# Padding small tiles of a two-layer decoder trunk so that its matmul operands start at multiples of 512 bytes

## The chip, the core and the metric

The kernel runs on one core of one Trainium2 chip. The metric is the device time of one execution in microseconds; less is better. Before the change it is 2253.3 us, the median of 3 runs (2253.23 to 2253.68).

## What is computed

Two layers of a decoder on 256 tokens with 2048 features, all inputs and outputs fp32. Layer 0 mixes tokens with sparse attention ("NSA"), layer 1 with gated linear attention ("GLA"); each is followed by an MLP with a hidden width of 8192.

```python
def squared_relu_mlp(h, w_up, w_down):
    return jnp.square(jax.nn.relu(h @ w_up)) @ w_down

def reference(x, ...):
    for i in range(DEPTH):                      # DEPTH = 2
        h = rms_norm(x, norm_mix[i])
        y = nsa_mixer(h, ...) if i == 0 else gla_mixer(h, ...)
        x = x + y
        h = rms_norm(x, norm_mlp[i])
        x = x + squared_relu_mlp(h, mlp_w_up[i], mlp_w_down[i])
    return x
```

Every mixer begins with one wide projection (h @ w_in) and ends with another (@ w_out). These projections and the MLPs are the "dense products"; what lies between them (scores, softmax, decays, transposes) is small.

## The kernel before

**Precision.** A dense product of fp32 numbers is made from three products of a shorter fp32 form (the type F32R): each operand is split into a high part and a low part, and high by high, high by low and low by high are summed in PSUM. The split of a weight tile is a copy on ScalarE (`wh`) and a subtraction on VectorE (`wl`), lines 194 and 198; the activations `op` (and the hidden activations `ht` of the MLP) lie in SBUF with the high and the low part side by side.

**Stages and loops.** In time: NSA projections with the attention worked in between (`mode_a`: the activations are stationary, 512 weight columns move, three matmuls for each 128 rows and 128 tokens); the NSA output projection (`out_proj`: weights stationary, 256 activation columns move); the first MLP (`mode_b` with `wide`: weights stationary; one matmul moves 512 columns, the high and the low part of the activations, and one moves 256); then GLA's projections, its output projection and the second MLP in the same forms. The MLP takes its 8 chunks of hidden features in turn: up 0, up 1, down 0, up 2, down 1, and so on. The hidden activations of the even chunks lie in tiles `ht` of the pool `mlpz`, those of the odd chunks in tiles `op` of the pool `opool`.

**Order.** All instructions are issued in an order that a planner in the program (`Plan`) fixes when the program is built: the dense products are the main line, and the steps of attention and of the norms step in between them. The weights come through the queue of SyncE in loads of 1 MB, three of them in flight (`raw`).

**Where tiles lie.** Pools lie in each partition of SBUF in the order in which they are opened, and tiles of a pool one behind the other; every tile starts at a multiple of 32 bytes. In bytes from the start of a partition the order is: constants (`cid` at 16512, 768 bytes; `mhalf` at 17280), `xpool` (the residual stream `xs`), `opool` (7 tiles `op`), `wraw` (`raw`), `wsp` (`wh`, `wl`), `small` (vectors such as `rstd`), `zpool`, and behind that the pools of a layer (`mlpz`, or `nsa1` and `nsa2`, or `gla1` and `gla2`). `mhalf` is 8 fp32 wide, 32 bytes, so that `xs0` begins at 17312, which is 33 * 512 + 416. All tiles of `xpool`, `opool`, `wraw` and `wsp` are whole multiples of 512 bytes long, so all of them begin 416 bytes behind a multiple of 512.

The lines that issue every product of the main line:

```python
    def mm(dst, lhsT, rhs, **kw):
        ...
        nc.tensor.matmul(dst, lhsT, rhs, skip_group_check=True, **kw)
```

`lhsT` is the stationary operand, which is loaded into the array by an instruction of its own (LDWEIGHTS, engine PEld in the profile), and `rhs` the moving one. Each matmul has its own weight load.

Of the kernel before, what the change touches and what calls it, by code (L numbers as in the profile page):

```python
# [10 lines left out]
F32 = mybir.dt.float32  # L11
# [7 lines left out]
P = 128  # L19
T = 256  # L20
# [11 lines left out]
class Plan:  # L32
    """Order of emission, which every engine keeps. The dense products are the main line; side
    streams (generators) step in between their matmuls. A stream yields (time, resources): when
    its next step's operands are there, by the plan's clocks, and the slots this step takes."""
# [10 lines left out]
    # -- operands  # L46
# [16 lines left out]
    # -- slots of the pools  # L63
# [17 lines left out]
    # -- streams  # L81
# [32 lines left out]
    def wait(self, needs):  # L114
        """For the main line: let the streams give slots back."""
        while not all(sum(f < 1e12 for f in self.slots[tag]) >= n for tag, n in needs.items()):
            self.tick(1e9)
            self.t["pe"] += 50.0
# [3 lines left out]
def trunk_kernel(ctx: ExitStack, tc: tile.TileContext, a: dict, out: bass.AP):  # L122
# [108 lines left out]
    def evac_splits(items):  # L231
        """evac_split of several, whose low parts don't hold up the vector engine."""
        for hi, lo, src, scale in items:
            if scale is None:
                copy(hi, src)
            else:
                act(hi, src, AF.Copy, scale=scale)
        yield W.ready(items[-1][0])
        for hi, lo, src, scale in items:
            if scale is None:  # L240
                tt(lo, src, hi.bitcast(F32), ALU.subtract)
            else:
                stt(lo, src, scale, hi.bitcast(F32), ALU.mult, ALU.subtract)
# [19 lines left out]
    def slotted(pool, tag, n):  # L263
        """An allocator of a pool's slots which the plan knows of."""
        W.pool(tag, n)

        def alloc(shape, dtype=F32):
            t = pool.tile(list(shape), dtype, tag=tag, name=nm(tag), bufs=n)
            W.take(tag, t)
            return t  # L270
        return alloc
# [12 lines left out]
    mhalf = const.tile([P, 8], F32, name="mhalf")  # L284
    nc.gpsimd.memset(mhalf, -0.5)
    # the scalar engine's table and the tensor engine's clock, while the first loads are under way
    idle = zpool.tile([P, T], F32, tag="junk", name="idle")
    nc.vector.memset(idle, 0.0)
    copy(mhalf[:, 7:8], mhalf[:, 0:1])
# [4 lines left out]
    # by features: [128, tokens] each  # L294
    xs = [xpool.tile([P, T], F32, name=f"xs{n}") for n in range(KT)]

# [1 line left out]
    class Weights:  # L298
        AHEAD = 2
        # when the plan expects the first half units  # L300
# [109 lines left out]
    # the first two units of an MLP: first halves before second ones  # L410
# [11 lines left out]
    def mode_a(op, ps, kts, before=None):  # L422
        """ps[t] = sum over kts of x^T(kt)[tok, :] @ w(kt); a half unit holds 2 kt."""
        k0, k1 = kts[0], kts[-1]
        for i in range(0, len(kts), 2):
            pair = kts[i:i + 2]
            if before is not None:
                for kt in pair:
                    before(kt)
            hi, lo = weights.next()  # L430
            for t in range(NT):
                for j, kt in enumerate(pair):
                    wh = hi[:, j * 512:(j + 1) * 512]
                    wl = lo[:, j * 512:(j + 1) * 512]
                    o = op[kt // 4]
                    xh = o[:, kt % 4, 0, t * P:(t + 1) * P]
                    xl = o[:, kt % 4, 1, t * P:(t + 1) * P]
                    mm(ps[t], xh, wh, start=(kt == k0), stop=False)
                    mm(ps[t], xh, wl, start=False, stop=False)
                    mm(ps[t], xl, wh, start=False, stop=(kt == k1))  # L440
                    if t == 0 and j == 1:
                        weights.lows()
                    W.tick()
                    weights.early()

    def mode_b(op, steps, wide, before=None, slack=2500.0):
        """A half unit, 8 of w(kt)^T @ x(kt) for 128 features each; wide: the low parts' products
        in ps[:, T:]. Steps: kt, ps, first and last of its sum."""
# [18 lines left out]
    def out_proj(oTs, after, ready):  # L467
        """Halves of K; in them blocks of 8 features, whose sums take two turns of 4 kt each."""
# [24 lines left out]
    def gate_product(op):  # L493
        """[96, T]: products with the weights' high and low parts in turn."""
# [18 lines left out]
    def transposed(src, cols):  # L513
        """A bank [128, 2, NT, 128] with the transposes of two column blocks of src [128, NT, 512]."""
        pt = aux([P, 2, NT, P])
        for j, c in enumerate(cols):
            for t in range(NT):
                transpose(pt[:, j, t, :], src[:, t, c:c + P], ident)
        return pt

    class Prep:
        """Gained operand of the next phase, and the tokens' mean squares."""
# [50 lines left out]
        def rstd(self):  # L573
            """Per token, which are on the partitions."""
# [10 lines left out]
            r = small.tile([P, NT], F32, tag="rstd", name=nm("rstd"))  # L585
# [3 lines left out]
    def mlp(prep, after, last):  # L589
        op = prep.op  # L590
        with tc.tile_pool(name="mlpz", bufs=2) as zp:
# [4 lines left out]
            def factors():  # L596
                """1 / mean square of every token, on all partitions."""
# [85 lines left out]
    # ================= layer 0: NSA =================  # L683
    def nsa(prep, after):
        op = prep.op
        G, HPG = 4, 4
        with tc.tile_pool(name="nsa1", bufs=1) as s1, tc.tile_pool(name="nsa2", bufs=1) as s2:
# [7 lines left out]
            def tables():  # L695
                """Constants, and the rope tables with the gains: (cos*g, swapped sin*g)."""
# [12 lines left out]
                gcol = s1.tile([P, 4], F32, name="gcol")  # L709
# [8 lines left out]
                vsel = s1.tile([48, 2], F32, name="vsel")  # L718
# [23 lines left out]
            def factors():  # L742
                rstd = yield from prep.rstd()
                # rstd^2 / 128, rstd / 2
                r2d = s1.tile([P, NT], F32, name="r2d")
                tt(r2d, rstd, rstd, ALU.mult)
                ts(r2d, r2d, 1.0 / P, None, ALU.mult)
                rhalf = s1.tile([P, NT], F32, name="rhalf")
# [3 lines left out]
            # columns: first tokens' selection and window keys, compressed ones, the other tokens'  # L752
# [10 lines left out]
            def normed(dst, ps):  # L763
                """dst = heads of 128 over their rms (with the tokens' factors)."""
# [39 lines left out]
            def keys(ps, g0):  # L804
                """A block of keys: selection and window branch of the groups g0 and g0 + 1."""
# [23 lines left out]
            def compress(ps, which):  # L829
# [18 lines left out]
                def fetch(u):  # L848
                    # u in turn into a slot of either pool
# [9 lines left out]
                for u in range(4):  # L859
# [16 lines left out]
                    # high and low parts side by side, of the weights and of the blocks  # L876
# [80 lines left out]
                else:  # L957
                    # rows 0..16 and 32..48: high part; rows 16..32: low part
# [57 lines left out]
            def attend(g, h, qT, oT):  # L1016
# [19 lines left out]
                # per query and branch: largest score, negated  # L1036
# [11 lines left out]
                # p: [cmp 16, 16 | sel 0, win 0 of the first tokens | sel 0, win 0, sel 1, win 1 of the others]  # L1048
# [38 lines left out]
                # compressed branch: high, high, low parts side by side  # L1087
# [7 lines left out]
                # transposed probabilities: [sel0 256 | win0 256], [sel1 128 | win1 128 | cmp 256]  # L1095
# [68 lines left out]
    # ================= layer 1: GLA =================  # L1164
    def gla(prep, after):
        op = prep.op
        NLEV = 8
        with tc.tile_pool(name="gla1", bufs=1) as s1, tc.tile_pool(name="gla2", bufs=1) as s2:
# [10 lines left out]
            onorm = s1.tile([P, 4], F32, name="onorm")  # L1179
# [7 lines left out]
            # blocks of 64 tokens: the high parts on one half of the partitions, the low parts on the other  # L1187
# [18 lines left out]
            def factors():  # L1206
                rstd = yield from prep.rstd()
                rq = s1.tile([P, NT], F32, name="rq")
                ts(rq, rstd, 1.0 / 16.0, None, ALU.mult)
                rhalf = s1.tile([P, NT], F32, name="rhalf2")  # L1210
# [3 lines left out]
            def decays():  # L1214
                # three rows of 32 of each: high, low, high by high, high, low
# [84 lines left out]
            def attn(hd, kq, dg, wait, res):  # L1300
                """Exponents of a level: first halves of its blocks, then second ones. att[:, 0/1]: both token
                tiles by themselves, att[:, 2]: second queries on first keys."""
# [3 lines left out]
                for cc in range(2):  # L1306
# [3 lines left out]
                    for t in range(NT):  # L1310
                        yield 0.0, {"aux": 1}
                        # levels 0 and 1: of a tile
# [36 lines left out]
                # level 1: first half on second; level 2: the same in both halves  # L1349
# [19 lines left out]
                # the others within halves of a tile, first by query: 32 queries of a level and tile to a row block  # L1369
# [53 lines left out]
            def swish(ps):  # L1423
                """(tanh(r/2) + 1) * r, without the token's factor rstd/2 on the last r."""
# [106 lines left out]
def _units_a(w):  # L1531
    """[K, N] -> [N/512, K/512, 128, 4*512]: blocks of 512 columns, units of 4 x 128 rows."""
    k, n = w.shape
    return w.reshape(k // 512, 4, P, n // 512, 512).transpose(3, 0, 2, 1, 4).reshape(n // 512, k // 512, P, 2048)


def _units_b(w):
    """[2048, 2048] -> [16, 128, 2*1024]: halves of K, blocks of 8 x 128 columns, quarters of K; half units
    of 2 x 128 columns by 4 x 128 rows."""
# [3 lines left out]
def _cols_b(w):  # L1543
    """[2048, M] -> [128, 16*M]"""
# [3 lines left out]
def _constants():  # L1548
# [31 lines left out]
    # cumulative sums: level l halves blocks of 256 >> l tokens; right: mid..t, left: t+1..mid-1  # L1580
    cum = np.zeros((P, 2, 8, P), np.float32)
    s = np.arange(P)
    for t in range(2):
        for l in range(8):
            hs = 128 >> l
            for col in range(P):
                # in the order of the exponents
# [9 lines left out]
    # by blocks of 64 tokens, twice: levels 0, 1, 0 of the tiles' first ones, of the second ones; the other levels  # L1597
# [68 lines left out]
```

## Time and profile before

| | |
|---|---|
| time, median of 3 runs | 2253.3 us |
| span of the profiled execution | 2249.9 us |
| around the span (median less span) | 3.4 us |
| TensorE busy | 2242.6 us, 13171 matmuls |
| weight loads busy (beside the matmuls) | 1964.8 us |
| VectorE busy | 1612.9 us |
| ScalarE busy | 1124.5 us |
| chain that ended last | 99% TensorE |

The page gives busy times on the slowest core; here there is only one. An execution's own time is its span, from the first to the last instruction, and what lies around it; the page gives the span, and 3.4 us is what the median of the runs has beyond it. A matmul's length in the profile has the time until its last result lands, so that lengths of neighbours overlap: how many a microsecond the engine does is read from their starts, or from the pieces of the chain (length by count).

### The profile page before, as it was taken

To read this page: it belongs to the slowest core of one execution; us is meant where nothing else is said; L and a number is where in the kernel's file an instruction comes from. 1 tells how busy PE (TensorE), PEld (TensorE's weight loads), DVE (VectorE), ACT (ScalarE), POOL (GpSimd) and SP (SyncE) were. 2 spreads that over 40 slices of the span, in tenths; PEclk is the share of its full clock that TensorE was granted. 3 is DMA by queue.
4 is the path that set the end of the run, shared out by engine and by line. 5 is a ranking of instruction groups with operands and counts; after the bars stand their busy time and mean duration, and the time that the engine had idled before them with its cause. 6 is when DMAs were issued, how large, how long until landed. Compare 5 with 4: busy or idle time off the path is not lost.

```text
span 2249.9 us, 33393 instructions
## 1 busy us (share of the span) xinstructions
PE 2242.6 (100%) x13171; PEld 1964.8 (87%) x13171; DVE 1612.9 (72%) x2646; ACT 1124.5 (50%) x1886; POOL 30.0 (1%) x43
## 2 busy tenths in 40 slices
PE   9999999999999999999999999999999999999999
PEld 7888899988888888888888888899888888888888
DVE  6778677777777777777966656667777777777776
ACT  6567676544444444444565555445444444444443
POOL 0010000000000000000000000000000000000000
PEclk9999999999999999999999999999999999999999
DMA  7644333555555555555654444455555555555554
GB/s 257 226 175 146 127 117 135 186 186 190 192 193 193 188 187 187 190 190 194 219 176 168 150 171 149 164 176 184 187 190 192 193 193 187 187 187 190 190 194 156
DMA packets 63453, 408.55 MB, mean 182 GB/s; under 512 B 8256, under 2 KB 13008, under 8 KB 15424
## 3 DMA queue, kind: packets, MB, share of 16 engines
q1 hardware_dynamic: 62416, 403.78, 50.4%
q0 software_dynamic: 880, 2.64, 0.5%
q8 instruction: 103, 1.69, 0.3%
q14 instruction: 54, 0.44, 0.1%
HBM read 403.25 MB, written 2.10 MB: 180 GB/s over the span
## 4 chain that ended last, share of the span: by engine, by line
PE 99%; DVE 1%; DMA 0%; SPq 0%; issue 0%; ACT 0%; DVEq 0%
PE psa L163 61%; PE psx L163 37%; PE psx L167 1%; DMA raw<-in_nsa_in_dram 0%; DVE att L1400 0%; DVE wl L198 0%; DVE op L202 0%; SPq L1514 0%; DVE g L202 0%; ACT wh L194 0%; SPq L324 0%; DVE xs L198 0%; DVE ath L198 0%; SPq L281 0%; DVEq L202 0%
## 5 line engine op out<-in xcount | busy, mean ns | idle before, releaser
L194 ACT CAST wh<-raw 128x1024 fp32r<-128x1024 f32 (+1 forms) x757 | 793.7, 1049 | 689.1 <-PE psa L163 564.4
L198 DVE TENSOR_TENSOR wl<-raw,wh 128x1024 fp32r<-128x1024 f32 (+1 forms) x753 | 920.3, 1222 | 283.5 <-ACT wh L194 261.4
L163 PE MATMUL psx<-op,wh 128*128 128x512 f32 (+1 forms) x2080 | 722.3, 393 | 0.0
L163 PE MATMUL psx<-op,wl 128*128 128x256 f32 x2048 | 573.9, 280 | 0.0
L163 PE MATMUL psa<-op,wh 128*128 128x512 f32 (+1 forms) x2048 | 541.6, 337 | 0.0
L163 PE MATMUL psa<-wh,op 128*128 128x512 f32 x1408 | 470.0, 397 | 2.1 <-ACT wh L194 2.1
L163 PEld LDWEIGHTS psx<-op,wh 128*128 128x128 f32 (+1 forms) x2080 | 388.6, 187 | 89.0
L163 PE MATMUL psa<-op,wl 128*128 128x256 f32 x1536 | 431.6, 281 | 0.0
L163 PEld LDWEIGHTS psa<-op,wh 128*128 128x128 f32 x2048 | 351.1, 189 | 42.9
L163 PEld LDWEIGHTS psx<-op,wl 128*128 128x128 f32 x2048 | 387.0, 189 | 0.1
L163 PE MATMUL psa<-ht,wh 128*128 128x512 f32 x1024 | 355.4, 390 | 0.0
L198 DVE TENSOR_TENSOR xs<-xs,psa 128x256 f32<-128x256 f32 x576 | 239.6, 421 | 151.7 <-PE psa L163 142.7
L163 PEld LDWEIGHTS psa<-wh,op 128*128 128x128 f32 x1408 | 264.9, 188 | 58.1 <-ACT wh L194 2.5
L163 PEld LDWEIGHTS psa<-op,wl 128*128 128x128 f32 x1536 | 291.6, 190 | 0.0
L163 PE MATMUL psa<-ht,wl 128*128 128x256 f32 x1024 | 288.8, 282 | 0.0
L163 PE MATMUL psa<-wl,op 128*128 128x512 f32 x704 | 275.5, 391 | 0.3 <-DVE wl L198 0.3
L163 PEld LDWEIGHTS psa<-ht,wh 128*128 128x128 f32 x1024 | 192.2, 188 | 40.4
L163 PEld LDWEIGHTS psa<-ht,wl 128*128 128x128 f32 x1024 | 193.5, 189 | 0.0
L194 ACT COPY zt<-psx 128x256 f32<-128x256 f32 x128 | 47.6, 372 | 222.9 <-PE psx L163 222.9
L163 PEld LDWEIGHTS psa<-wl,op 128*128 128x128 f32 x704 | 132.8, 189 | 23.9 <-DVE wl L198 1.6
L198 DVE TENSOR_TENSOR zz<-psx,zt 128x256 f32<-128x256 f32 x128 | 54.4, 425 | 116.4 <-ACT zt L194 116.4
L202 DVE SCALAR_TENSOR_TENSOR zr<-zz 128x256 f32<-128x256 f32 x128 | 54.4, 425 | 4.4
(186 smaller groups left out, 1123.3 us busy)
## 6 DMA issues: line engine op xcount, KB each, us to landing
raw<-in_mlp_up_dram SPq DMA_DIRECT2D x128, 1024.0 KB, 4.8
raw<-in_mlp_down_dram SPq DMA_DIRECT2D x128, 1024.0 KB, 4.8
raw<-in_gla_in_dram SPq DMA_DIRECT2D x48, 1024.0 KB, 4.8
raw<-in_nsa_in_dram SPq DMA_DIRECT2D x38, 1024.0 KB, 4.8
raw<-in_nsa_out_dram SPq DMA_DIRECT2D x16, 1024.0 KB, 4.8
raw<-in_gla_out_dram SPq DMA_DIRECT2D x16, 1024.0 KB, 4.8
xs<-in_x_dram SPq DMA_DIRECT2D x16, 128.0 KB, 4.8
pT<-in_cmp_w_dram SPq DMA_DIRECT2D x4, 512.0 KB, 5.6
```

The lines of the kernel that those rows point to most:

```text
L163: nc.tensor.matmul(dst, lhsT, rhs, skip_group_check=True, **kw)
L167: nc.tensor.transpose(dst, src, idn)
L194: nc.scalar.copy(dst, src)
L198: nc.vector.tensor_tensor(dst, x, y, op=op)
L202: nc.vector.scalar_tensor_tensor(dst, x, s, y, op0=op0, op1=op1)
```

## The change

Ten small tiles get more columns; where a tile had 2 or 4 columns, the program now takes a wider one and uses the first 2 or 4 of it. The comments and docstrings of the file go too, and leave blank lines; they are not shown.

```diff
-    mhalf = const.tile([P, 8], F32, name="mhalf")
+    mhalf = const.tile([P, 32], F32, name="mhalf")
     nc.gpsimd.memset(mhalf, -0.5)
...
-    copy(mhalf[:, 7:8], mhalf[:, 0:1])
+    copy(mhalf[:, 31:32], mhalf[:, 0:1])
...
-            r = small.tile([P, NT], F32, tag="rstd", name=nm("rstd"))
+            r = small.tile([P, 16], F32, tag="rstd", name=nm("rstd"))[:, 0:NT]
             rpow(r, ms)
...
-                gcol = s1.tile([P, 4], F32, name="gcol")
+                gcol = s1.tile([P, 32], F32, name="gcol")[:, 0:4]
...
-                vsel = s1.tile([48, 2], F32, name="vsel")
+                vsel = s1.tile([48, 16], F32, name="vsel")[:, 0:2]
...
-                r2d = s1.tile([P, NT], F32, name="r2d")
+                r2d = s1.tile([P, 32], F32, name="r2d")[:, 0:NT]
...
-                rhalf = s1.tile([P, NT], F32, name="rhalf")
+                rhalf = s1.tile([P, 32], F32, name="rhalf")[:, 0:NT]
...
-            onorm = s1.tile([P, 4], F32, name="onorm")
+            onorm = s1.tile([P, 24], F32, name="onorm")[:, 0:4]
...
-                rq = s1.tile([P, NT], F32, name="rq")
+                rq = s1.tile([P, 32], F32, name="rq")[:, 0:NT]
...
-                rhalf = s1.tile([P, NT], F32, name="rhalf2")
+                rhalf = s1.tile([P, 32], F32, name="rhalf2")[:, 0:NT]
```

No instruction is added, removed or moved on any engine. One has another size: the memset of `mhalf` fills 32 columns and not 8. What differs otherwise is where tiles lie in SBUF (bytes from the start of a partition, and their distance from the multiple of 512 below):

| tiles | before | after | use in the dense products |
|---|---|---|---|
| xs0 to xs15 | 17312 .. (416) | 17408 .. (0) | none (residual stream) |
| op, 7 tiles | 33696 .. (416) | 33792 .. (0) | moving, in mode_a stationary |
| raw | 91040 .. (416) | 91136 .. (0) | none (source of the split) |
| wh, wl | 115616 .., 127904 .. (416) | 115712 .., 128000 .. (0) | stationary, in mode_a moving |
| ht, 2 tiles | 152000, 160192 (448) | 152192, 160384 (128) | moving, down projection of even chunks |
| qT (NSA) | 206848 .. (0) | 207360 .. (0) | not dense: stationary |
| pT (NSA) | 200704 (0) | 201216 (0) | not dense: moving |
| kT0 to kT3 (NSA) | 150464 .. (448, 64, 192, 320) | 150656 .. (128, 256, 384, 0) | not dense: moving |
| vv0, vv1 (NSA) | 167360, 175552 (448) | 167552, 175744 (128) | not dense: stationary |

Between two tiles of `xpool`, `opool`, `wraw` and `wsp` the distance is what it was, since all of them move by 96 bytes. `zpool`, `mlpz` and the first tiles of the layers' pools move by 192. The gate products read a `wh` tile in pieces of 384 bytes, so that their stationary operand starts at another distance from a multiple of 512 in each of eight products in a row.

## Rows read from the trace of the kernel before

**Rows 1.** The page, busy time by engine and granted clock in 40 slices.

```profile
PE 2242.6 (100%) x13171; PEld 1964.8 (87%) x13171; DVE 1612.9 (72%) x2646; ACT 1124.5 (50%) x1886; POOL 30.0 (1%) x43
...
PEclk9999999999999999999999999999999999999999
```

**Rows 2.** What TensorE waited for (us in total, times, longest).

```profile
PE psa L163 <- ACT wh L194: 2.1, 1, 2.1
...
PE psa L163 <- DVE wl L198: 0.3, 1, 0.3
```

**Rows 3.** Window of the first MLP: length, busy time (count) by engine, clock, DMA.

```profile
500.00:1032.00 532.00, 532.00 (x3071) 469.70 (x3070) 388.30 (x576) 234.80 (x288) 0.00 (x0) 1.00 0.54 190
```

**Rows 4.** Groups by shape: busy, mean of one; a product stands as moving,stationary.

```profile
L198 DVE TENSOR_TENSOR wl<-raw,wh 128x1024 fp32r<-128x1024 f32 x751 | 919.0, 1224 | 283.5 <-ACT wh L194 261.4
...
L163 PE MATMUL psx<-op,wh 128*128 128x512 f32 x2048 | 714.5, 393 | 0.0
...
L163 PE MATMUL psa<-wh,op 128*128 128x512 f32 x1408 | 470.0, 397 | 2.1 <-ACT wh L194 2.1
L163 PE MATMUL psa<-op,wl 128*128 128x256 f32 x1536 | 431.6, 281 | 0.0
...
L163 PE MATMUL psa<-ht,wh 128*128 128x512 f32 x1024 | 355.4, 390 | 0.0
```

**Rows 5.** Chain that ended last: start, length (us), count of consecutive matmuls.

```profile
104.38 3.73 PE psx L163 x16
...
500.27 44.38 PE psa L163 x256
...
589.03 44.37 PE psa L163 x256
...
1310.03 21.11 PE psa L163 x93
...
1454.99 79.19 PE psa L163 x660
```

**Rows 6.** Timeline of TensorE, a dense pair of the MLP: start, length (us).

```profile
599.96 0.39 PE L163 MATMUL psa<-op,wh 128*128 128x512 f32 x1
600.19 0.28 PE L163 MATMUL psa<-op,wl 128*128 128x256 f32 x1
600.31 0.39 PE L163 MATMUL psa<-op,wh 128*128 128x512 f32 x1
```

**Rows 7.** Timeline of TensorE, stationary tile qT, moving tile op.

```profile
70.73 0.39 PE L163 MATMUL psa<-wh,op 128*128 128x512 f32 x1
70.96 0.63 PE L163 MATMUL psx<-op,qT 128*128 128x256 f32 x4
71.44 0.40 PE L163 MATMUL psa<-wh,op 128*128 128x512 f32 x1
```

**Rows 8.** Timeline of TensorE, stationary qT with moving kT, then moving pT.

```profile
193.05 0.77 PE L163 MATMUL psx<-kT,qT 128*128 128x256 f32 x5
193.66 0.29 PE L163 MATMUL psx<-maskr,identr 128*128 128x272 f32 x1
193.78 0.29 PE L163 MATMUL psx<-kT,qT 128*128 128x272 f32 x1
193.90 0.40 PE L163 MATMUL psa<-wh,op 128*128 128x512 f32 x1
...
194.60 0.52 PE L163 MATMUL psx<-pT,vv 128*128 128x256 f32 x3
```

**Rows 9.** Timeline of TensorE, the kT products beside the output projection.

```profile
353.56 0.77 PE L163 MATMUL psx<-kT,qT 128*128 128x256 f32 x5
...
354.43 0.39 PE L163 MATMUL psa<-op,wh 128*128 128x256 f32 x2
```

**Rows 10.** Timeline of the start, all engines.

```profile
0.74 0.10 POOL L285 MEMSET mhalf<- 128x8 f32 x1 [0.29 <-POOLq L1656]
...
7.48 0.80 PE L163 MATMUL psa<-wh,op 128*128 128x512 f32 x1 [2.06 <-ACT wh L194]
```

## The prediction

> **What bounds the kernel now.** I read the page first. TensorE is busy for 2242.6 of 2249.9 us, at a granted clock of nine tenths or more of full speed in all 40 slices [rows 1]; the level is thus 2.4 GHz, not 1.2. A matmul's busy time runs past the start of the next one, so 100% busy doesn't yet say that nothing is left to win. The waits say that nobody keeps the engine: the two longest entries for a dense product are 2.1 and 0.3 us in the whole run [rows 2]. The window of the first MLP shows why: in 532 us VectorE works for 388.3 us and ScalarE for 234.8 us [rows 3]. So only the rate of TensorE itself sets the time, and a change of addresses counts where it changes that rate.
>
> The rate is read from the pieces of the chain, length by count [rows 5]. In the output projection, where every matmul moves 256 columns, 660 take 79.19 us, 120.0 ns each. In GLA's projection, where every one moves 512, 93 take 21.11 us, 227.0 ns each. 256 columns more cost 107.0 ns, or 0.418 ns a column, which is one column per cycle at 2.4 GHz. What is left does not depend on the columns: 120.0 - 106.7 = 13.3 ns, and 227.0 - 213.3 = 13.7 ns. The MLP's pair (512 and 256 columns) agrees: 256 matmuls in 44.38 us are 346.7 ns a pair, and 346.7 - 320.0 is twice 13.3 ns. The starts of one pair lie 0.23 and 0.12 us apart [rows 6], so no single matmul hides a stall. Thus each dense matmul pays 13.3 ns, some 32 cycles, beside its columns. If the position of its operands has a price, it lies in these 13.3 ns.
>
> How many pay it [rows 4]: 2048 pairs of up (op,wh), 1024 pairs of down from ht, and 1024 from op (of the 1536 op,wl products 512 belong to the output projections, which issue three matmuls for each: 1536). The projections in front have 1408 wh,op, two of three: 2112. In all 8192 + 1536 + 2112 = 11,840 matmuls, which take 4096 * 0.3467 + 1536 * 0.1200 + 2112 * 0.2270 = 2084 us of the 2249.9. The part beside the columns is 8192 * 13.3 + 1536 * 13.3 + 2112 * 13.7 ns = 158 us. That is the most that the change can give.
>
> **What the change does, step by step.** No instruction is added, removed or moved, so no wait is either. (1) The memset of mhalf has 32 columns for 8. The one before takes 0.10 us at 0.74 us, and the first dense product starts at 7.48 us, held by the cast of the first weights [rows 10]. Four times the columns can cost at most four times 0.10 us, and 6.6 us of load hide it. Cost: 0. (2) The padded vectors (rstd, gcol, rq and the others) are read and written with the same 2 or 4 elements, from one row of a partition each. Cost: 0. (3) raw, wh, wl, op and xs move by 96 bytes as written by DMA, ScalarE and VectorE. The split of a half weight tile takes VectorE 1224 ns [rows 4]; what hides a loss there is the idle 27% of VectorE in the MLP [rows 3], so its work would have to slow by 532 / 388.3, 37%, before TensorE waited. Cost: 0, and no gain, as nobody waits for it. (4) The matmuls read operands at 0 in place of 416 bytes behind a multiple of 512. This is the only step with a price, and the trace can bound it, because it has tiles at other places.
>
> *Moving operand.* The down projection of chunk 0 moves ht, which begins at 448; that of chunk 1 moves op, at 416; the stationary weights are the same. 256 matmuls take 44.38 us with the one and 44.37 us with the other [rows 5]. One is a multiple of 64 bytes, the other is not, and it costs 0.04 ns. A moving operand that is a full multiple of 512 before the change is pT. Three products with it take 0.52 us from the first start to the last end [rows 8]; less the 0.28 us that a matmul of 256 columns takes to its own end [rows 6] these are two intervals of 0.12 us, the dense rate again.
>
> *Stationary operand.* qT is a multiple of 512. Four products with it, moving op from 416, fill 70.96 to 71.44 us, 0.12 us each [rows 7], as in the output projection. Seven with moving kT (three of 256 columns and four of 272, 1856 columns, 773 ns) fill 193.05 to 193.90 us [rows 8], and that leaves 77 ns, 11.0 each; the same seven at 353.56 us take 0.87 us [rows 9], 13.8 each. The timeline is rounded to 10 ns, so that these are 11 to 14, in the mean 12.4: at most 1 ns below the dense 13.3.
>
> So a multiple of 512 on one side alone buys between 0 and 1 ns a matmul, and I take 0, because the cleanest rows (ht against op, and 256 matmuls each) say 0.04. Both sides at once is not in this trace; that stays open and is a rival. The sum: 2249.9 + 0 + 0 + 0 + 0 = 2249.9 us of span, and with the 3.4 us around it **2253.3 us**, no change.
>
> A rule that speaks for a gain: the Trainium skill, "TensorE: Matmul & The Clock Gate", section "Back-to-back issue gap", gives columns / 2.4 + 2.5 ns from matmul to matmul, for single ones, warm. This trace disagrees with it, with 13.3 ns for the 2.5 [rows 5]. If the difference were the price of the operands' places, and the change gave it back, the sum would be, as an estimate from that page, 11,840 * 10.8 ns = 128 us less, 2125 us. A second page, "SBUF — State Buffer", section "Operand start alignment", asks only for a multiple of the element's size and says that its rule is about legality and not speed; by it nothing changes.
>
> **The rivals.** *A. Both operands must be aligned, and then the 13.3 ns go.* The weight load and the moving stream would each be slow at 416, and either alone enough to set the rate. For it: the 32 cycles are the same everywhere, and no dense product has had both aligned. Against it: ht and pT on the moving side and qT on the stationary side would each have had to meet a partner that costs just as much. At most 158 us go: 2095 us; half of it would be 2174 us. Chance 0.10.
>
> *B. The stationary operand's place matters a little.* The 1 ns of the kT rows, if it is qT's place and not jitter, on 11,840 matmuls is 12 us: 2241 us. For it: the mean of two runs; against it: the op,qT products at 0.12 us. Chance 0.12.
>
> *C. Slower: the distance between two operands matters.* It stays the same for op and the weights, but for ht and the weights it goes from 32 to 128 bytes. The row for this is the gate product, the only one whose operands lie at a changing distance (its weights advance by 384 bytes): 16 take 3.73 us [rows 5], 233.1 ns each for 512 columns, 6.5 ns more than the pair's rate. The cause may as well be that its stationary operand has 96 columns. On the 2048 ht matmuls 6.5 ns are 13 us: 2266.6 us. It decides from 2.2 ns on, where 0.2% (4.5 us) is reached. Against it: the 32 bytes of before cost 0.04 ns. Chance 0.10; other losses of this kind, in the attention products whose tiles move against each other, 0.06 more.
>
> *D. The change has no effect* is the forecast itself, chance 0.60; 0.02 remain for gains that I have no mechanism for.
>
> **The numbers.** About 0.2% is what a measurement of this kernel can tell from no change. Faster by more than that is A, B and the rest, 0.24; slower 0.16; the same 0.60. The range reaches from B's 2240 to C's 2267 us and leaves out A and the far part of C, some 0.15. The forecast's own range is 2249 to 2258 us, since its bound on both sides is 0.2%.
>
> **What would show it.** If right, the stretches of 256 in the chain stay at 44.4 us for op and for ht, the gap at 256 columns at 120 ns and at 512 columns at 227 ns, and the counts and waits don't change. If A holds, a stretch of 256 falls towards 128 * 320 ns = 41.0 us; if B, to about 44.1 us; if C, only those with ht rise, to 44.4 + 256 * 6.5 ns = 46.0 us. A gain without shorter stretches would have to come out of the attention stages, and would mean that I misjudged a wait there. What makes me wrong most easily is A: the trace holds no dense product with both operands on a multiple of 512.

## The result and the profile after

The changed kernel takes 2270.99 us (median of 4 runs, 2270.31 to 2272.11) against 2253.34 us for the kernel before (median of 4): 17.65 us slower, ratio 1.0079, 95% interval 1.0065 to 1.0094. I had forecast no change.

The page of the changed kernel answers to [rows 1]:

```profile
span 2269.4 us, 33393 instructions
...
PE 2261.8 (100%) x13171; PEld 1965.5 (87%) x13171; DVE 1612.7 (71%) x2646; ACT 1123.8 (50%) x1886; POOL 29.2 (1%) x43
...
PEclk9999999999999999999999999999999999999999
```

TensorE is busy 19.2 us longer with the same count at the same granted clock; VectorE and ScalarE work as long as before. Its waits for dense products are 2.1 and 0.7 us, for 2.1 and 0.3 [rows 2]. So nothing waits more: matmuls follow one another more slowly. Where, the chain shows (start, length, count), first in the changed kernel:

```profile
1320.38 21.11 PE psa L163 x93
...
1465.27 79.20 PE psa L163 x660
1544.47 89.36 PE psx L163 x514
1633.83 44.94 PE psa L163 x256
1678.76 45.22 PE psx L163 x256
1723.99 45.23 PE psa L163 x256
```

and then in the kernel before, the pieces of the second MLP that were not among [rows 5]:

```profile
1534.18 90.89 PE psx L163 x514
1625.07 44.38 PE psa L163 x256
1669.45 44.38 PE psx L163 x256
1713.83 44.37 PE psa L163 x256
```

GLA's projection (93 matmuls in 21.11 us) and the output projection (660 in 79.20 us) have the rate of before, 227.0 and 120.0 ns, although their operands moved by the same 96 bytes. Only the MLP's pairs changed, and in both directions. The stretch that an MLP begins with (up 0 and up 1) got faster, 89.36 for 90.89 us. Behind it everything got slower: the down chunks that read ht by 0.56 us a stretch, all others by 0.85. That is -1.53 + 4 * 0.56 + 10 * 0.85 = 9.2 us an MLP and 18.4 for both; the rest of the span's 19.5 us, 1.1 us, lies ahead of the first MLP, which begins at 410.52 and not 409.38 us. That part differs from run to run: x1_mhalf_only, below, begins its first MLP at 410.58 us and takes as long as the kernel before.

The row that I had overlooked stands in the second fence, and it stands in the first MLP too, right ahead of the stretch at 500.27 us [rows 5]:

```profile
409.38 90.89 PE psx L163 x514
```

514 matmuls in 90.89 us are 353.7 ns a pair, while the same form, with op tiles and weight tiles at the same distances from multiples of 512, takes 346.7 ns from the next stretch on. So the kernel before already had two rates at one set of places, and it changed between them at 1625 us, where the moving tile changes from op to ht for the first time. The changed kernel runs most of its first piece at the fast rate (it begins with some 25 slow pairs) and leaves that rate where ht is read first. Its stretches with ht have a rate of their own, 44.94 us or 351.1 ns a pair, which the kernel before doesn't show.

The timeline shows what the slow rate is. Starts of the kernel before in its slow stretch (start, length):

```profile
430.14 0.40 PE L163 MATMUL psx<-op,wh 128*128 128x512 f32 x1
430.38 0.28 PE L163 MATMUL psx<-op,wl 128*128 128x256 f32 x1
430.49 0.40 PE L163 MATMUL psx<-op,wh 128*128 128x512 f32 x1
430.73 0.28 PE L163 MATMUL psx<-op,wl 128*128 128x256 f32 x1
430.84 0.40 PE L163 MATMUL psx<-op,wh 128*128 128x512 f32 x1
431.08 0.28 PE L163 MATMUL psx<-op,wl 128*128 128x256 f32 x1
431.20 0.40 PE L163 MATMUL psx<-op,wh 128*128 128x512 f32 x1
```

and of the changed kernel, behind the first down chunk:

```profile
559.84 0.40 PE L163 MATMUL psx<-op,wh 128*128 128x512 f32 x1
560.07 0.28 PE L163 MATMUL psx<-op,wl 128*128 128x256 f32 x1
560.19 0.40 PE L163 MATMUL psx<-op,wh 128*128 128x512 f32 x1
560.43 0.28 PE L163 MATMUL psx<-op,wl 128*128 128x256 f32 x1
560.55 0.40 PE L163 MATMUL psx<-op,wh 128*128 128x512 f32 x1
560.79 0.28 PE L163 MATMUL psx<-op,wl 128*128 128x256 f32 x1
560.90 0.40 PE L163 MATMUL psx<-op,wh 128*128 128x512 f32 x1
```

Three pairs take 1.06 us in both, with unequal gaps, where the fast rate has 0.35 us from pair to pair [rows 6]. It is one slow rhythm of three pairs, 353.3 ns each, and both kernels have it at some time in stretches that read op.

### The profile page after: what moved, and what is told of

It reads as the page before. It is cut to its first block, busy times and chain, and to the rows that moved or that the text cites. A ratio compares the mean times of both kernels' runs of the same rounds, so it can differ in the third digit from the quotient of the medians.

```text
span 2269.4 us, 33393 instructions
## 1 busy us (share of the span) xinstructions
PE 2261.8 (100%) x13171; PEld 1965.5 (87%) x13171; DVE 1612.7 (71%) x2646; ACT 1123.8 (50%) x1886; POOL 29.2 (1%) x43
## 4 chain that ended last, share of the span: by engine, by line
PE 99%; DVE 1%; DMA 0%; SPq 0%; issue 0%; ACT 0%; DVEq 0%
PE psa L163 61%; PE psx L163 37%; PE psx L167 1%; DMA raw<-in_nsa_in_dram 0%; DVE att L1400 0%; DVE wl L198 0%; DVE op L202 0%; SPq L1514 0%; DVE g L202 0%; ACT wh L194 0%; SPq L324 0%; DVE xs L198 0%; DVE ath L198 0%; SPq L281 0%; DVEq L202 0%
## 5 line engine op out<-in xcount | busy, mean ns | idle before, releaser
L163 PE MATMUL psa<-op,wh 128*128 128x512 f32 (+1 forms) x2048 | 548.5, 341 | 0.0
L198 DVE TENSOR_TENSOR zr<-zr,r 128x256 f32<-128x256 f32 x128 | 54.4, 425 | 4.4
```

The lines of the kernel that those rows point to most:

```text
L198: nc.vector.tensor_tensor(dst, x, y, op=op)
```

## The experiments

Theory R, which I formed from these rows: at the same places the pair stream has a fast and a slow rhythm. It keeps the one it is in until something disturbs it, and which one follows depends on the step in SBUF from the operands of before to the next. Theory A is the rival: a start at a multiple of 512 costs some 6 ns a pair. Theory D: any shift draws the rhythm anew, without a rule.

**The two parts of the change by themselves.** Widening mhalf moves everything behind it by 96 bytes; widening rstd moves what lies behind it by another 96. So each alone separates the place of op and the weights from the step between op and ht. (The diff has nine widened tiles, not ten; the other seven lie in the pools of the two mixers.) The first is x1_mhalf_only:

```diff
-    mhalf = const.tile([P, 8], F32, name="mhalf")
+    mhalf = const.tile([P, 32], F32, name="mhalf")
```

> Only mhalf is widened (to 32 columns): op, wh, wl, raw and xs start at a multiple of 512 as after the change, but ht starts at 32, so that the step from op to ht is 32 bytes as before the change (after the change it is 128). Theory R (two rhythms: at the same places a pair of the MLP takes 346.7 or about 353 ns; which one holds is settled where the moving tile changes from op to ht, by the step between them, 32 bytes to the fast one and 128 to the slow one): as before, 2253 us, pairs of 346.7 ns from the first down chunk on. Theory A (the place itself: a start at a multiple of 512 costs some 6 ns a pair): 2271 us, pairs of 352 to 353 ns. Theory D (any shift draws the rhythm anew, without a rule): either, or stretches of both.

Measured: 2252.61 us, ratio to the kernel before 1.0000, 0.9991 to 1.0010. Every stretch is that of the kernel before, 90.89 and then 44.37 or 44.38 us.

The second is x2_rstd_only:

```diff
-            r = small.tile([P, NT], F32, tag="rstd", name=nm("rstd"))
+            r = small.tile([P, 16], F32, tag="rstd", name=nm("rstd"))[:, 0:NT]
```

> Only rstd is widened (to 16 columns): op, wh, wl, raw and xs start 416 behind a multiple of 512 as before the change, ht at 32, so that the step from op to ht is 128 bytes as after it. Theory R: slow, 2271 us, pairs of 351 to 353 ns from the first down chunk on. Theory A: 2253 us. Theory D: either.

Measured: 2270.55 us, ratio 1.0081, 1.0066 to 1.0096, with op and the weights at 416 as before. The chain of this kernel has the stretches of the changed one:

```profile
410.50 89.36 PE psx L163 x514
499.86 44.94 PE psa L163 x256
544.79 45.22 PE psx L163 x256
590.02 45.23 PE psa L163 x256
```

Theory A falls twice over: with the multiples of 512 alone nothing is lost, and without them everything is. What costs comes with the padding of rstd, which sets 128 bytes between op and ht. Theory D falls as well: x1_mhalf_only repeats the kernel before and x2_rstd_only the changed one, stretch by stretch, with op and the weights elsewhere.

**No step at all (x3_no_step).** In the kernel before, unused space ahead of ht brings it to op's distance from a multiple of 512:

```diff
             r2 = zp.tile([P, T], F32, tag="r2", name=nm("r2"), bufs=1)
+            zp.tile([P, 120], F32, tag="gap", name=nm("gap"), bufs=1)
```

> The kernel before with 480 bytes of unused space ahead of ht, so that op and ht both start at 416: no step between them. Theory R: nothing changes the rhythm that the MLP begins with (353.3 ns in the kernel before until the first down chunk), so all 4096 pairs are slow: 3584 more than before, 6.67 ns each, 24 us, 2277 us. If the first switch is not from the step but from another event at that place: 2253 us. Theory A: 2253 us.

Measured: 2276.48 us (one run, as for all that follow but x5_fast_kept) against 2252.4 for the kernel before beside it, 24.1 us more. The slow rhythm that the MLP begins with is never left:

```profile
410.37 90.89 PE psx L163 x514
501.26 45.22 PE psa L163 x256
546.48 45.23 PE psx L163 x256
591.71 45.23 PE psa L163 x256
```

This shows that it is ht's place relative to the others that ends the slow rhythm in the kernel before, and not the change of bank, of stage or of a wait there, which are all still there. I call it the step from op to ht. It could as well be the distance of ht from the weights, since the weights lie at op's distance from a multiple of 512; no run separates the two.

**The fast rhythm kept (x5_fast_kept).** The same in the changed kernel, which comes to ht in the fast rhythm:

```diff
             r2 = zp.tile([P, T], F32, tag="r2", name=nm("r2"), bufs=1)
+            zp.tile([P, 96], F32, tag="gap", name=nm("gap"), bufs=1)
```

> The changed kernel with 384 bytes of unused space ahead of ht, so that op and ht both start at a multiple of 512. Theory R: both MLPs come into the fast rhythm a few half tiles after their start, as in the changed kernel (stretch of 89.36 us for 90.89), and no step ever takes them out of it: every stretch of 256 at 44.37 us, and 2 times 1.5 us less than the kernel before, 2250 us. Theory A (a multiple of 512 costs 6 ns a pair): 2271 to 2276 us.

Measured: 2249.6 us (median of 11 runs), ratio to the kernel before 0.9986, 0.9977 to 0.9995, some 3.3 us faster than before and 21 faster than the change. Op and the weights lie at multiples of 512 here, and every stretch is fast:

```profile
409.23 89.36 PE psx L163 x514
498.59 44.37 PE psa L163 x256
542.96 44.37 PE psx L163 x256
587.34 44.37 PE psa L163 x256
```

**A break that moves nothing (x4_extra_matmul).** The changed kernel with a small matmul ahead of each down chunk, whose result the next matmul overwrites:

```diff
                     ps = acc1()
+                    if f == 0:
+                        nc.tensor.matmul(ps[:, 0:32], ident, ident[:, 0:32], skip_group_check=True, start=True, stop=True)
```

> The changed kernel with one needless small matmul (32 columns, overwritten by the next one) ahead of each of the 16 down chunks; all places are as after the change. Theory R: the break lets a rhythm start anew, so that some stretches fall back to 346.7 ns a pair, which no place explains; between 2253 and 2275 us. Theory A: every stretch of 256 stays at 44.9 us or more, and the time is 2271 plus 16 times 0.1 to 0.2 us, 2273 to 2274 us.

Measured: 2261.94 us, 9.5 us above the kernel before measured beside it where the changed kernel was 17.65 above, with 16 products more (32 instructions in the trace) and all tiles at its places:

```profile
544.29 45.22 PE psx L163 x256
589.65 44.46 PE psa L163 x256
634.11 44.37 PE psx L163 x256
678.63 45.01 PE psa L163 x256
```

The break ahead of a chunk that reads op (589.65) starts the fast rhythm, which lasts through the up chunk behind it; the break ahead of a chunk that reads ht starts a slow one. The up chunk at 544.29 and that at 634.11 read tiles at the same places and differ by 0.85 us: what differs is what ran before them.

**What starts the rhythm of an MLP.** In the fourth half tile of each MLP a product of two other tiles, sum (moving) and ones (stationary), stands between the pairs (issued in lines 602 and 163). Up to it both kernels take some 353 ns a pair; behind it the kernel before goes on slowly and the changed kernel goes on at 346.7 ns. I moved its two operands one at a time in x3_no_step, by 96 bytes; no other tile that a matmul reads changed its distance from a multiple of 512. First sum, in x9_sum_moved:

```diff
+            if self.which == 0:
+                zpool.tile([P, 24], F32, tag="gap1", name=nm("gap"))
             self.sum = zpool.tile([P, T], F32, tag="sum", name=nm("sum"))
+            if self.which == 0:
+                zpool.tile([P, 104], F32, tag="gap2", name=nm("gap"))
```

> The kernel x3_no_step (all pairs slow, 2276.5 us) with one tile moved by 96 bytes: sum, which is the moving operand of the two-instruction product with ones that stands between the fourth half tile's pairs at the start of each MLP. Its step from op becomes 128 bytes for 32, as in the changed kernel; every other tile stays where it was, modulo 512. Theory R: that product starts the rhythm anew, and with the step of 128 it starts the fast one, which nothing ends, since op and ht have no step: stretches of 44.37 us, first stretch 89.36, 2250 us, 27 us less than x3. If the first rhythm comes from elsewhere: 2276 us.

Measured: 2277.37 us. Every stretch stayed slow, so my expectation failed: moving the moving operand of that product by 96 bytes did nothing.

Then ones, in x10_ones_moved (the tile r2 moves with it, which no matmul reads):

```diff
+            zp.tile([P, 24], F32, tag="gap0", name=nm("gap"), bufs=1)
             ones = zp.tile([P, P], F32, tag="ones", name=nm("ones"), bufs=1)
...
-            zp.tile([P, 120], F32, tag="gap", name=nm("gap"), bufs=1)
+            zp.tile([P, 96], F32, tag="gap", name=nm("gap"), bufs=1)
```

> The same with ones moved by 96 bytes, the stationary operand of that product, and sum left at its place. Theory R1 (the step of the moving operand decides): slow as x3, 2276.5 us. Theory R2 (the stationary operand's place decides as well): fast, 2250 us.

Measured: 2250.26 us, 27 us less than x9_sum_moved beside it and 26 less than x3_no_step, from 96 bytes in the place of one small tile that two matmuls of each MLP read:

```profile
411.13 89.36 PE psx L163 x514
500.50 44.37 PE psa L163 x256
544.87 44.37 PE psx L163 x256
589.24 44.37 PE psa L163 x256
```

Here the stationary operand's place decides; between op and ht, where the weights stay, it is the moving one's. It fits the other runs: ones lies 1536 bytes ahead of ht in the kernel before and in the changed one, so at 32 bytes from op's distance before and at 128 after. With 32 the first piece took 90.89 us and with 128 it took 89.36, in every run in which the low weights stayed.

**Other steps from op to ht (x11_step_64, x12_step_256).** In the changed kernel, with 112 and 32 columns of unused space in the line of x5_fast_kept:

> The changed kernel with ht 64 bytes behind a multiple of 512, a step of 64 from op (x5 has 0, the changed kernel 128). The MLP comes to the first down chunk in the fast rhythm. Theory R gives no rule for 64: either it stays at 44.37 us a stretch, 2250 us, or the step ends it, 45.0 to 45.2 us a stretch, 2271 us.

> The changed kernel with ht 256 bytes behind a multiple of 512. As for x11: 2250 us if a step of 256 keeps the rhythm, 2271 us if it ends it like the step of 128.

Measured: 2272.43 us with a step of 64 bytes, 2250.22 with 256. At 64 the first stretch with ht takes 44.66 us and all behind it 45.22, those with ht too; at 256 all take 44.37.

```profile
500.01 44.66 PE psa L163 x256
544.67 45.22 PE psx L163 x256
...
680.35 45.22 PE psa L163 x256
```

The stretches at 500.01 and 680.35 read the same tiles ht, 348.9 and 353.3 ns a pair: again the sequence, not the place. And there are more than two rates: with the 351.1 ns of the changed kernel's stretches with ht, the runs show at least four, some 2.2 ns a pair apart. So steps of 0 and 256 kept the fast rhythm, 64 and 128 ended it, and 32 kept it in the kernel before.

With the rows of ht 2080 bytes apart, in x5_fast_kept (x7_ht_rows_32):

```diff
-                            ht = zp.tile([P, 4, 2, T], F32R, tag="ht", name=nm("ht"))
+                            ht = zp.tile([P, 4, 520], F32R, tag="ht", name=nm("ht"))
+                            ht = ht[:, :, 0:2 * T].rearrange("p k (a t) -> p k a t", a=2)
```

> As x5_fast_kept, but with the rows of ht 2080 bytes apart in place of 2048, so that the moving operand steps by 32 bytes from each pair to the next in the down chunks that read ht. Theory R: the rhythm of those chunks changes, since each pair makes a step, and what they leave behind is found in the up chunks after them; a pair between 340 and 360 ns. If only the step at the change of tiles counts, because it comes with the change of the PSUM bank or of a wait: 346.7 ns everywhere, 2250 us.

Measured: 2273.35 us; the chunks with ht take 44.9 us a stretch, and all that follow are left at 45.2. The fast rhythm does not survive rows that lie 0, 32, 64 and so on to 224 bytes from op's distance. Which of them ends it the run doesn't tell: 64 and 128, which end it by themselves, are among them.

**The low weights moved (x6_wl_64, x8_wl_32).** In x3_no_step, with wl 64 or 32 bytes further on than wh (the numbers for 64):

```diff
     mhalf = const.tile([P, 8], F32, name="mhalf")
+    small.tile([P, 112], F32, tag="gap", name=nm("gap"), bufs=1)
...
+                if i == 0:
+                    wsp.tile([P, 16], F32, tag="gap", name=nm("gap"), bufs=1)
                 lo = wsp.tile([P, 1024], F32R, tag="wl", name=nm("wl"))
```

> The kernel without a step between op and ht (x3), with wl 64 bytes further on than wh (480 for 416 behind a multiple of 512); everything behind wl stays where it was, modulo 512. Theory R1 (only steps of the moving tile matter): 353.3 ns a pair as in x3, 2276.5 us. Theory R2 (the step of the stationary tile from wh to wl and back counts as well): another rhythm, between 340 and 360 ns a pair.

> As x6_wl_64, with wl 32 bytes further on. Theory R1: 353.3 ns a pair, 2276.5 us. Theory R2: another rhythm than x3 has, and perhaps another than x6_wl_64.

Measured: 2252.82 and 2254.51 us, 24 and 22 us less than x3_no_step. The stationary side's steps count as well (R2): no slow rhythm is left in either MLP. But neither is clearly faster than the kernel before (2252.92 us beside them), as x5_fast_kept is, and the chain of x6_wl_64 says why:

```profile
1313.12 21.58 PE psa L163 x93
...
1459.34 77.75 PE psa L163 x660
1537.08 89.19 PE psx L163 x514
1626.28 44.37 PE psa L163 x256
```

The output projection got faster, 117.8 ns a matmul for 120.0, and GLA's projection, where wh and wl are the moving operand, got slower, 232.0 for 227.0 [rows 5]. The same move thus helps one product and slows another.

## Why the prediction was wrong

**What bounds the kernel** was right: TensorE's rate, no wait, same clock. Steps 1 to 3 (memset, padded vectors, the split) show no cost, as said: VectorE 1612.7 us, ScalarE 1123.8.

**The step that failed** is the fourth, the bound on the operands' places. I compared ht with op in two stretches of the kernel before, 44.38 and 44.37 us, and concluded that the moving operand's place costs 0.04 ns. Both stretches were in the fast rhythm, so the comparison could not show that there is another. I took the rate for a property of the operands' places; it is one of the sequence. The term that I put at 0 came to 18.4 us in the two MLPs. The evidence was in the same view, the piece of 514 matmuls in 90.89 us right ahead of the stretch that I quoted: 353.7 ns a pair for op at the same 416. I had accounted for 4096 pairs at 346.7 ns and never asked for that piece. The readings of qT, pT and kT then tested places in runs of 3 to 7 matmuls, too short to say which rhythm they would settle in; and one of the seven matmuls counted for qT moves maskr over identr [rows 8].

**The rivals.** C had the right tile and the right sign: the distance of ht from the weights (and from op) goes from 32 to 128 bytes, and x5_fast_kept and x12_step_256, which move ht again and nothing that a matmul reads besides, win the whole loss back. Where the cost falls it had wrong. It charged the ht matmuls with 6.5 ns each, 13 us; in fact a stretch with ht loses 0.56 us, while the stretches with op, whose distances did not change at all, lose 0.85 us each, since the rhythm outlasts the step. So its sum missed the larger share, and its price, 6.5 ns from the gate product, is not the one measured: a pair of these matmuls loses 4.4 ns, and the gate product itself takes 3.73 us before and after. A and B (a multiple of 512 gives something back) fall with x1_mhalf_only: 0 us. The rule of the Trainium skill, "TensorE: Matmul & The Clock Gate", section "Back-to-back issue gap", by which, for single matmuls, 2.5 ns would remain beside the columns, is met by no long stretch of any run: the least at 256 columns is 11.1 ns (77.75 us by 660, in x6_wl_64). And the Trainium skill's "SBUF — State Buffer", section "Operand start alignment", speaks of legality and not of speed; these runs show that a tile's place, legal in both cases, is worth 27 us (x9_sum_moved and x10_ones_moved).

**What is open.** Why there are several rhythms, what sets 32, 64, 128 and 256 bytes apart, and whether the step from op or the distance from the weights counts, no run here tells; that the reads of the weights and of the moving operand meet in SBUF would be a guess. Nor do I know why the products with 256 or 512 columns alone, in the projections, have kept one rate through the change, though wl's place moves it.

## What to carry to other kernels

A back-to-back stream of matmuls can run at more than one rate with the same instructions on tiles at the same places, up to 2% apart here; before a rate is taken for a property of the operands, look in the chain for stretches of the same form that differ. A change that only moves tiles in SBUF is a change of the steps between tiles, and its effect can be far from what moved: compare stretches one by one, and undo the parts separately. Tiles that alternate as an operand of a stream kept the rhythm they came with when they lay at the same distance from a multiple of 512, but that is no remedy by itself: it kept the fast one in x5_fast_kept and the slow one in x3_no_step, the fastest and nearly the slowest kernel of all these. Which layout is fast has to be measured.

## What was not expected of the hardware

The pair of 512 and 256 columns takes 346.7 ns or 353.3 ns at 2.4 GHz with its tiles at the same places (kernel before, up stretches at 1534 and 1669 us), and keeps either for hundreds of microseconds: 24 us lie between x3_no_step and the kernel before, in nothing but that. A product that takes some 0.25 us (sum by ones, in the changed kernel), or one with 32 columns (x4_extra_matmul), is enough to switch it.
